# Retention's output product: the third and fourth column pairs each in two banks of the other PSUM pool, all four pairs in the wide form

## The chip, the cores and the metric

The kernel runs on one core of one Trainium2 chip. The metric is device time in microseconds (us) of one execution, the median over several runs. A profile is one execution taken by the hardware profiler: it gives every instruction with its engine, its line of the kernel, its tiles, its start and its duration.

## The reference

The reference is a trunk of four layers over 256 tokens of width 1024, batch 1. Each layer adds a token mixer and then a squared-ReLU MLP to the residual stream:

```python
for i in range(DEPTH):            # DEPTH = 4
    kind = i % N_MIXERS           # 0 retention, 1 convolution, 2 stick-breaking attention
    h = rms_norm(x, norm_mix[i])
    m = mixer[kind](h)
    x = x + m
    x = x + squared_relu_mlp(rms_norm(x, norm_ffn[i]), ffn_w1[i], ffn_w2[i])
return rms_norm(x, final_norm)
```

Retention is the mixer of layers 0 and 3. It ends with `return (jax.nn.silu(g) * y) @ w_out`, a product of a 256 x 2048 activation with a 2048 x 1024 weight. That product is the place of the change. It is followed in both layers by the MLP, whose first product is `h = relu(xn @ w1)` with a 1024 x 4096 weight.

## The kernel before, in words

Everything is float32. A float32 factor is split into a high part and a low part, and a product of two factors is taken as three partial products: high weight with high activation, high weight with low activation, low weight with high activation. Activations lie transposed: a tile of 128 partitions holds 128 features, its columns 0 to 255 are the high part of the 256 tokens, its columns 256 to 511 the low part.

**Weights** come in units of 512 KB (128 partitions x 1024). `unit` (L325) brings two units with one DMA on the SP queue into a `raw` tile, ScalarE casts the high part `wh` (L350, 128x1024), VectorE subtracts and leaves the low part `wl` (L357, 128x1024). `wh` and `wl` come from a pool of five buffers each (`wp`), taken in turn: the cast of a unit waits until TensorE has read the unit five places earlier for the last time. A unit of kind "b" holds four blocks of 128 rows by 256 columns, that is, one column pair (two output tiles of 128 features).

**Two forms** of a product on such a unit. The narrow form, `mm_b` (L490), makes three matmuls of 256 columns for each block of rows and each output tile (L504, L505, L506) and puts both output tiles of the pair into one PSUM bank. The wide form, `mm_w` (L509), makes two: the low weight with the 256 high columns (L520) and the high weight with all 512 columns at once (L524). It needs a bank for each output tile, since high and low part of the activation land in different halves; `sum_w` (L562) adds the halves afterwards: for each of the two banks a copy on ScalarE (L567) and an addition on VectorE (L568).

**PSUM** has eight banks here in two pools of four, `acc` and `mis`, each taken in turn. `acc` serves the large products; `mis` serves transposes, the attention products, column sums and broadcasts. A new tile waits until its bank has been read by all who read it before.

**The output product of retention** (L873 to L882): four column pairs, p = 0 to 3, each over 16 blocks of rows, which are four units (kb = 0 to 3). `OUT_ORDER` takes pairs 0 and 1 alternately through kb 0 to 3, and then pairs 2 and 3 the same way. Pairs 0, 1 and 2 are in the wide form with two `acc` banks each, pair 3 in the narrow form with one `acc` bank. When a pair is done, `evac` (L889) adds it to the residual x (L892), and `norm_pair` makes the two split activation tiles z of the next product (L439 on ScalarE, L440 on VectorE) and squares x (L450); GpSimd adds the squares up (L455).

**The MLP's first product** (`ffn`, L602) reads all eight z tiles; the last two, from pair 3, are here called z6 and z7. It has 16 pairs over two units each. In layer 0 all pairs are wide. In layer 3 the first two are narrow with one bank each and are evacuated only when the norm's factor is known; column sums (L400) give the mean square, VectorE finds its inverse root in eight small instructions (L469 and L384 to L395), and TensorE broadcasts it (L407). In layer 0 a sum over partitions (L480) takes that place.

**Order.** Most of the program's order is set by the compiler's scheduler, which simulates the engines and takes what it holds to be ready first; on each engine the instructions then run in that order. Only some matmuls are kept in program order by hand. A change in one place can therefore move instructions around it.

Of the kernel before, what the change touches and what calls it, by code (L numbers as in the profile page):

```python
# [242 lines left out]
class Trunk:  # L243
# [474 lines left out]
    def retention(self, j, nxt):  # L718
# [4 lines left out]
        q, k = [], []  # L723
        cosb, sinb = self.b2(self.c("cos", S)), self.b2(self.c("sin", S))
        for h in range(RH):
            for isk in range(2):
                if j == h == 0:
                    if not isk:
                        first = self.pairs_qk("ret_w_in", j, 0)
                    ps = first[isk]  # L730
                else:
                    ps = (self.pair_w if j else self.pair_b)("ret_w_in", j, isk * D + h * DK, self.zs)
# [55 lines left out]
        for h in range(RH):  # L788
            pv = [self.acc(), self.acc()]
            for kb in range(4):  # L790
                w = self.unit(("ret_w_in", j, "a", kb, 2 * D + h * DV))
# [14 lines left out]
            ps = self.mis()  # L806
# [18 lines left out]
        y = []  # L825
        for h in range(RH):
# [29 lines left out]
            for kb in range(4):  # L856
                w = self.unit(("ret_w_in", j, "a", kb, 4 * D + h * DV))
# [15 lines left out]
        evac = self.out_begin(nxt)  # L873
        ps = {}
        for kb, p in OUT_ORDER:
            w = self.unit(("ret_w_out", j, "b", kb, p * 256))
            two = p < 3
            if kb == 0:
                ps[p] = (self.acc(), self.acc()) if two else self.acc()
            (self.mm_w if two else self.mm_b)(ps[p], w, lambda k: y[k], kb * 4, kb == 0, kb == 3)  # L880
            if kb == 3:
                evac(p, self.sum_w(ps[p]) if two else ps[p])  # L882


    def out_begin(self, nxt, bias=None):
# [674 lines left out]
```

## Time and profile before

| what | value |
|---|---|
| runs of the kernel before | 1341.48, 1343.08, 1344.0 us (median 1343.08) |
| the profiled execution, first to last instruction (span) | 1340.3 us |
| median of the runs minus that span | 2.8 us |
| granted TensorE clock, mean | 0.999 |
| TensorE (PE) busy | 1330.8 us, 99% |
| VectorE (DVE) busy | 984.0 us, 73% |
| ScalarE (ACT) busy | 781.3 us, 58% |
| GpSimd (POOL) busy | 134.0 us, 10% |

The time of the profiled execution is known as its span only; the runs are 1.2 to 3.7 us longer than it.

A row of the timeline reads: start in us from the span's start, duration in us from the first to the last of the merged instructions, engine, line, operation, output tile <- input tiles, shape, how many instructions (x4), and in brackets the idle time before it and who ended that. Matmuls are pipelined: their durations overlap, and what one costs TensorE is the distance from its start to the next one's start. PEld rows are the weight loads of the matmuls.

### The profile page before, as it was taken

What the parts mean: (1) busy time and instruction counts of PE and PEld (TensorE: products, weight loads), DVE (VectorE), ACT (ScalarE), POOL (GpSimd) and SP (SyncE); (2) the same over time, 40 slices, a digit from 0 to 9 for tenths busy, and PEclk for the clock granted to TensorE, in tenths of its full rate; (3) what the DMA queues carried; (4) which work ended last, traced back from release to release, by engine and by line L of the source; (5) the groups of instructions that cost most, each with busy time, mean ns of one, the idle gap of its engine ahead of it and who ended that gap; (6) DMA issues with size and microseconds to landing.
All of it is one profiled execution on the core that took longest, in us unless ns stands there. A gap on an engine that the chain in (4) does not pass through costs nothing.

```text
span 1340.3 us, 20902 instructions
## 1 busy us (share of the span) xinstructions
PE 1330.8 (99%) x8285; PEld 1170.4 (87%) x8285; DVE 984.0 (73%) x1642; ACT 781.3 (58%) x1205; POOL 134.0 (10%) x123
## 2 busy tenths in 40 slices
PE   9999999999999999999999999999999999999998
PEld 7988888888999998888878898888888888988886
DVE  6977769775688698765687587755697777788643
ACT  7555546664457477744578577744565555555442
POOL 3200002000169210000100010000120000100000
PEclk9999999999999999999999999999999999999999
DMA  7555555555545645555453345555555454555551
GB/s 283 210 184 190 187 181 197 189 188 189 188 159 145 219 170 203 190 192 192 172 183 126 126 166 190 192 190 194 177 181 187 174 188 173 189 189 189 204 188 63
DMA packets 41586, 244.56 MB, mean 182 GB/s; under 512 B 4624, under 2 KB 9104, under 8 KB 14096
## 3 DMA queue, kind: packets, MB, share of 16 engines
q1 hardware_dynamic: 40768, 240.86, 50.7%
q10 hardware_dynamic: 720, 2.36, 0.5%
q8 instruction: 65, 1.06, 0.3%
q14 instruction: 33, 0.27, 0.1%
HBM read 241.27 MB, written 1.93 MB: 181 GB/s over the span
## 4 chain that ended last, share of the span: by engine, by line
PE 99%; DMA 0%; ACT 0%; DVE 0%; issue 0%; SPq 0%
PE acc L524 34%; PE acc L520 18%; PE acc L683 6%; PE acc L918 6%; PE acc L920 6%; PE acc L919 6%; PE acc L504 4%; PE acc L505 4%; PE acc L506 4%; PE acc L1087 1%; PE acc L1220 1%; PE mis L809 1%; PE mis L870 1%; PE mis L400 0%; PE mis L1458 0%; PE acc L585 0%
## 5 line engine op out<-in xcount | busy, mean ns | idle before, releaser
L357 DVE TENSOR_TENSOR wl<-raw,wh 128x1024 fp32r<-128x1024 f32 (+1 forms) x440 | 546.5, 1247 | 242.8 <-ACT wh L350 236.4
L350 ACT CAST wh<-raw 128x1024 fp32r<-128x1024 f32 (+1 forms) x440 | 456.5, 1042 | 353.1 <-PE acc L524 164.8
L524 PE MATMUL acc<-z,wh 128*128 128x512 f32 x1120 | 387.4, 392 | 0.0
L520 PE MATMUL acc<-z,wl 128*128 128x256 f32 x1120 | 310.2, 281 | 0.0
L524 PE MATMUL acc<-big,wh 128*128 128x512 f32 x864 | 298.8, 392 | 0.0
L524 PEld LDWEIGHTS acc<-z,wh 128*128 128x128 f32 x1120 | 208.3, 187 | 44.7
L520 PE MATMUL acc<-big,wl 128*128 128x256 f32 x864 | 238.5, 280 | 0.5 <-DVE t L568 0.5
L520 PEld LDWEIGHTS acc<-z,wl 128*128 128x128 f32 x1120 | 211.1, 189 | 1.7
L524 PEld LDWEIGHTS acc<-big,wh 128*128 128x128 f32 x864 | 161.0, 187 | 34.8
L520 PEld LDWEIGHTS acc<-big,wl 128*128 128x128 f32 x864 | 162.4, 189 | 2.3 <-DVE t L568 1.3
L918 PE MATMUL acc<-wh,z 128*128 128x512 f32 x352 | 138.0, 392 | 0.0
L920 PE MATMUL acc<-wh,z 128*128 128x512 f32 x352 | 137.3, 390 | 0.0
L919 PE MATMUL acc<-wl,z 128*128 128x512 f32 x352 | 137.2, 390 | 0.0
L455 POOL TENSOR_TENSOR t<-t,t 128x512 f32<-128x512 f32 x23 | 36.2, 1573 | 893.7 <-ACT t L450 850.6
L567 ACT COPY t<-acc 128x256 f32<-128x256 f32 x176 | 61.8, 373 | 100.6 <-PE acc L524 99.3
L568 DVE TENSOR_TENSOR t<-acc,t 128x256 f32<-128x256 f32 x176 | 69.1, 421 | 34.9 <-ACT t L567 34.8
L683 PE MATMUL acc<-wh,big 128*128 128x512 f32 x256 | 79.3, 390 | 0.0
L920 PEld LDWEIGHTS acc<-wh,z 128*128 128x128 f32 x352 | 66.1, 188 | 14.7 <-issue 0.8
L918 PEld LDWEIGHTS acc<-wh,z 128*128 128x128 f32 x352 | 66.1, 188 | 14.1 <-issue 0.8
L919 PEld LDWEIGHTS acc<-wl,z 128*128 128x128 f32 x352 | 66.1, 188 | 13.1
L504 PE MATMUL acc<-z,wh 128*128 128x256 f32 x256 | 72.5, 284 | 0.0
L505 PE MATMUL acc<-z,wh 128*128 128x256 f32 x256 | 72.4, 283 | 0.0
(259 smaller groups left out, 1813.0 us busy)
## 6 DMA issues: line engine op xcount, KB each, us to landing
raw<-in_w SPq DMA_DIRECT2D x214, 1024.0 KB, 4.8
raw<-in_w SPq DMA_DIRECT2D x8, 512.0 KB, 8.9
big<-in_gn SPq DMA_DIRECT2D x16, 256.0 KB, 5.2
raw<-hd SPq DMA_DIRECT2D x8, 263.0 KB, 4.8
raw<-hd SPq DMA_DIRECT2D x8, 131.5 KB, 3.6
x<-in_x SPq DMA_DIRECT2D x4, 256.0 KB, 6.3
wh<-in_w ACTq DMA_DIRECT2D x2, 512.0 KB, 6.4
wl<-in_w ACTq DMA_DIRECT2D x2, 512.0 KB, 8.5
```

The lines of the kernel that those rows point to most:

```text
L350: nc.scalar.copy(hi[:, s], src[:, s])
L357: self.nc.vector.tensor_sub(lo[:, s], src[:, s], hi[:, s])
L504: nc.tensor.matmul(o, wh[:, kk, cs], ah, start=st, stop=False, **kw)
L505: nc.tensor.matmul(o, wh[:, kk, cs], al, start=False, stop=False, **kw)
L520: mm = nc.tensor.matmul(ps[m][:, :S], wl[:, kk, cs], a[:, :S], start=first and kk == 0, stop=False, **kw)
L524: nc.tensor.matmul(ps[m], wh[:, kk, cs], a, start=False, stop=last and kk == 3, **kw)
L567: nc.scalar.copy(o[:, s], ps[m][:, S:])
L568: nc.vector.tensor_add(o[:, s], ps[m][:, :S], o[:, s])
L683: self.tc.keep_in_program_order(nc.tensor.matmul(ps[t], l, r[:, kk], start=False, stop=kb * 2 + kk == 31 and n == 2, **kw))
L918: nc.tensor.matmul(ps[t], zh[:, s], wh[:, kk], start=k == 0, stop=False, skip_group_check=True)
L919: nc.tensor.matmul(ps[t], zh[:, s], wl[:, kk], start=False, stop=False, skip_group_check=True)
L920: nc.tensor.matmul(ps[t], zl[:, s], wh[:, kk], start=False, stop=k == 7, skip_group_check=True)
```

## The change

Pair 3 is computed in the wide form as the others are. Pairs 0 and 1 keep two `acc` banks each; pairs 2 and 3 take two `mis` banks each. Nothing else in the source differs.

```diff
         for kb, p in OUT_ORDER:
             w = self.unit(("ret_w_out", j, "b", kb, p * 256))
-            two = p < 3
             if kb == 0:
-                ps[p] = (self.acc(), self.acc()) if two else self.acc()
-            (self.mm_w if two else self.mm_b)(ps[p], w, lambda k: y[k], kb * 4, kb == 0, kb == 3)
+                bank = self.acc if p < 2 else self.mis
+                ps[p] = bank(), bank()
+            self.mm_w(ps[p], w, lambda k: y[k], kb * 4, kb == 0, kb == 3)
             if kb == 3:
-                evac(p, self.sum_w(ps[p]) if two else ps[p])
+                evac(p, self.sum_w(ps[p]))
```

The scheduler's order differs around this place in layers 0 and 3 on TensorE, VectorE and ScalarE, up to the fourth pair of the MLP's first product; the rows of GpSimd and of the SP queue stand as before. Names with numbers are tiles: `acc_` and `mis_` are PSUM banks, `wh_` and `wl_` a unit's high and low part, `big_` the split activations of the output product, `z_` those of the MLP.

First place, TensorE in layer 0, the end of pairs 0 and 1 (`acc_1766`, `acc_1767`, `acc_1788`, `acc_1789`) and the start of pair 2 (1968 and 1969). Before:

```order
L524 MATMUL acc_1766<-big_1757,wh_1892 128x512
L524 MATMUL acc_1767<-big_1757,wh_1892 128x512
L524 MATMUL acc_1788<-big_1757,wh_1926 128x512
L524 MATMUL acc_1789<-big_1757,wh_1926 128x512
L520 MATMUL acc_1968<-big_1331,wl_1965 128x256
L524 MATMUL acc_1968<-big_1331,wh_1964 128x512
```

Of the change:

```order
L520 MATMUL mis_1968<-big_1331,wl_1965 128x256
L524 MATMUL mis_1968<-big_1331,wh_1964 128x512
L520 MATMUL mis_1969<-big_1331,wl_1965 128x256
L524 MATMUL mis_1969<-big_1331,wh_1964 128x512
L520 MATMUL mis_1968<-big_1334,wl_1965 128x256
L524 MATMUL mis_1968<-big_1334,wh_1964 128x512
L520 MATMUL mis_1969<-big_1334,wl_1965 128x256
L520 MATMUL acc_1766<-big_1748,wl_1893 128x256
```

Before, pair 2 began behind the last matmul of pairs 0 and 1, in the bank of pair 0. Now it begins ahead of the last quarter of pairs 0 and 1, in banks of the other pool.

Second place, VectorE in layer 0, at the first pair of the MLP's first product, whose banks are `acc_2192` and `acc_2193` before and `acc_2166` and `acc_2167` in the change. Before (`wl_2341` is the second unit of the MLP's third pair, and its five-places-earlier unit is `wl_2197`, the first of the first pair):

```order
L440 SCALAR_TENSOR_TENSOR z_2182<-x_119,prm_90,z_2182 128x256
L440 SCALAR_TENSOR_TENSOR z_2185<-x_119,prm_90,z_2185 128x256
L357 TENSOR_TENSOR wl_2341<-raw_2312,wh_2340 128x1024
L568 TENSOR_TENSOR t_438_2236<-acc_2192,t_438_2236 128x256
L568 TENSOR_TENSOR t_438_2236<-acc_2193,t_438_2236 128x256
```

Of the change (`wl_2354` is the first unit of the fourth pair, and its five-places-earlier unit is `wl_2191`, the second of the first pair):

```order
L568 TENSOR_TENSOR t_428_2150<-mis_1990,t_428_2150 128x256
L568 TENSOR_TENSOR t_428_2150<-mis_1991,t_428_2150 128x256
L892 TENSOR_TENSOR x_119<-t_428_2150,x_119 128x512
L357 TENSOR_TENSOR wl_2315<-raw_2286,wh_2314 128x1024
L440 SCALAR_TENSOR_TENSOR z_2156<-x_119,prm_90,z_2156 128x256
L440 SCALAR_TENSOR_TENSOR z_2159<-x_119,prm_90,z_2159 128x256
L357 TENSOR_TENSOR wl_2354<-raw_2351,wh_2353 128x1024
L568 TENSOR_TENSOR t_440_2210<-acc_2166,t_440_2210 128x256
L568 TENSOR_TENSOR t_440_2210<-acc_2167,t_440_2210 128x256
```

The preparation of weights now stands one unit further ahead where the first pair's evacuation comes. On TensorE at the same place, before, the last matmuls of the first pair (2192, 2193) were followed by nine matmul pairs of the second pair and L480, and then by the third pair in new banks; of the change:

```order
L524 MATMUL acc_2166<-z_2159,wh_2190 128x512
L524 MATMUL acc_2167<-z_2159,wh_2190 128x512
L520 MATMUL acc_2225<-z_2159,wl_2250 128x256
L524 MATMUL acc_2225<-z_2159,wh_2249 128x512
L520 MATMUL acc_2226<-z_2159,wl_2250 128x256
L524 MATMUL acc_2226<-z_2159,wh_2249 128x512
L480 MATMUL mis_2293<-t_432_2164,cst 128x256
L520 MATMUL acc_2284<-z_1918,wl_2289 128x256
```

Two matmul pairs and L480 now stand between the first pair's end and the third pair, whose bank `acc_2284` is that of `acc_2166`.

Third place, VectorE in layer 3, the inverse root of the norm's factor (its input is L400's sum, its result `ry` is L407's input). Before:

```order
L357 TENSOR_TENSOR wl_12259<-raw_12211,wh_12258 128x1024
L469 TENSOR_SCALAR rm_12136<-mis_12131 128x2
L384 TENSOR_SCALAR ry_12138<-rm_12136 128x2
L388 TENSOR_TENSOR rt_12139<-ry_12138 128x2
L389 SCALAR_TENSOR_TENSOR rt_12139<-rt_12139,rm_12136 128x2
L390 SCALAR_TENSOR_TENSOR rt_12139<-rt_12139 128x2
L391 SCALAR_TENSOR_TENSOR ry_12138<-rt_12139,ry_12138 128x2
L357 TENSOR_TENSOR wl_12298<-raw_12295,wh_12297 128x1024
L393 TENSOR_TENSOR rt_12139<-ry_12138 128x2
L357 TENSOR_TENSOR wl_12318<-raw_12295,wh_12317 128x1024
L394 SCALAR_TENSOR_TENSOR rt_12139<-rt_12139,rm_12136 128x2
L395 SCALAR_TENSOR_TENSOR ry_12138<-rt_12139,ry_12138 128x2
```

Of the change:

```order
L357 TENSOR_TENSOR wl_12246<-raw_12243,wh_12245 128x1024
L469 TENSOR_SCALAR rm_12084<-mis_12079 128x2
L357 TENSOR_TENSOR wl_12266<-raw_12243,wh_12265 128x1024
L384 TENSOR_SCALAR ry_12086<-rm_12084 128x2
L388 TENSOR_TENSOR rt_12087<-ry_12086 128x2
L389 SCALAR_TENSOR_TENSOR rt_12087<-rt_12087,rm_12084 128x2
L390 SCALAR_TENSOR_TENSOR rt_12087<-rt_12087 128x2
L391 SCALAR_TENSOR_TENSOR ry_12086<-rt_12087,ry_12086 128x2
L357 TENSOR_TENSOR wl_12305<-raw_12302,wh_12304 128x1024
L393 TENSOR_TENSOR rt_12087<-ry_12086 128x2
L394 SCALAR_TENSOR_TENSOR rt_12087<-rt_12087,rm_12084 128x2
L395 SCALAR_TENSOR_TENSOR ry_12086<-rt_12087,ry_12086 128x2
```

Two weight subtractions stand between L469 and L395 in both. What moved is which units they are: the subtraction ahead of L469 is now of `wl_12246`, and its five-places-earlier unit (`wh_12051`, `wl_12052`) is read by TensorE up to the second row before L400. On TensorE, 38 narrow matmuls and four wide matmul pairs stood between L400 and L407 before; 11 narrow matmuls and four wide pairs stand there in the change.

## The prediction

> **What bounds the kernel now.** I read the page first, then the waits of TensorE, then the timeline around the two retention layers.
>
> ```profile
> span 1340.3 us, 20902 instructions
> PE 1330.8 (99%) x8285; PEld 1170.4 (87%) x8285; DVE 984.0 (73%) x1642; ACT 781.3 (58%) x1205; POOL 134.0 (10%) x123
> PE 99%; DMA 0%; ACT 0%; DVE 0%; issue 0%; SPq 0%
> PE mis L292 <- POOL t L270: 1.3, 1, 1.3
> PE mis L1394 <- ACT big L1464: 1.0, 1, 1.0
> PE acc L585 <- ACT wh L350: 0.6, 1, 0.6
> PE acc L520 <- DVE t L568: 0.5, 2, 0.2
> ```
>
> TensorE is busy 99% of the span and is 99% of the chain that ended last. The last four rows are all that it waits for: 3.4 us in the whole program. So there is little waiting to win, any matmul time saved counts in full, and any wait that TensorE does not have today is paid in full. The last of these rows is the only wait inside the change. It comes twice, once in each retention layer:
>
> ```profile
> 182.86 1.09 PE L524 MATMUL acc<-big,wh 128*128 128x512 f32 x4
> 184.18 0.38 PE L520 MATMUL acc<-big,wl 128*128 128x256 f32 x1 [0.23 <-DVE t L568]
> 192.26 0.28 PE L504 MATMUL acc<-big,wh 128*128 128x256 f32 x1
> 197.89 0.28 PE L506 MATMUL acc<-big,wl 128*128 128x256 f32 x1
> 198.01 0.28 PE L520 MATMUL acc<-big,wl 128*128 128x256 f32 x1
> 201.25 0.28 PE L520 MATMUL acc<-big,wl 128*128 128x256 f32 x1
> 203.83 0.40 PE L524 MATMUL acc<-big,wh 128*128 128x512 f32 x1
> 204.06 0.28 PE L504 MATMUL acc<-big,wh 128*128 128x256 f32 x1
> 206.94 0.28 PE L520 MATMUL acc<-z,wl 128*128 128x256 f32 x1
> 209.77 0.52 PE L520 MATMUL acc<-z,wl 128*128 128x256 f32 x3
> ```
>
> **What the change removes.** *The wait for pair 0's bank.* The four L524 from 182.86 take TensorE 4 x 0.23 us (0.23 is 203.83 to 204.06), so pair 2 could start at 183.79; it starts at 184.18. In the change pair 2 has banks of its own pool, last read by the attention products long before: 0.39 us gone, 0.78 in two layers.
>
> *The narrow form.* From 192.26 to 198.01 run 48 narrow matmuls: 0.120 us each, 0.359 for the three of one block and output tile. From 201.25 to 204.06 run eight wide pairs: 0.351 each. Pair 3 has 16 blocks and two tiles, 32 such groups a layer, 64 in all: 64 x 0.008 = 0.5 us. The durations of the rows (0.28 three times against 0.28 and 0.40) would promise far more, but they overlap; starts count. Bounds: eight wide pairs from 206.94 to 209.77 take 0.354 each (0.3 us in all); the nine from 215.06 to 218.18, below, 0.347 (0.8 us).
>
> The Trainium skill, "TensorE: Matmul & The Clock Gate", section "Back-to-back issue gap", gives N/2.4 + 2.5 ns between starts at full clock: an estimate from it is 327 ns for three narrow and 325 for a wide pair, so 0.15 us instead of 0.5. The rows show 359 and 351, and they decide.
>
> **What it adds.** Four ScalarE copies and four VectorE additions in all, 0.37 and 0.42 us each by the page. They delay z6 and z7. In the change 24 wide pairs (8.4 us) stand between the MLP's start and the first read of z6 in layer 0, and 64 narrow matmuls (7.7 us) in layer 3. VectorE's path to z6 is set by the subtraction ahead of it, whose buffer is free after the MLP's first unit: 2.8 + 0.4 for that unit, 1.04 cast, 1.25 subtraction, 0.76 for z6 (mean of L440, 46.5 us over 64), 6.3 us. It fits, so I cost them at nothing; without the cover one copy and one addition a layer would show, 0.8 us each time.
>
> ```profile
> L357 DVE TENSOR_TENSOR wl<-raw,wh 128x1024 fp32r<-128x1024 f32 (+1 forms) x440 | 546.5, 1247 | 242.8 <-ACT wh L350 236.4
> L350 ACT CAST wh<-raw 128x1024 fp32r<-128x1024 f32 (+1 forms) x440 | 456.5, 1042 | 353.1 <-PE acc L524 164.8
> L567 ACT COPY t<-acc 128x256 f32<-128x256 f32 x176 | 61.8, 373 | 100.6 <-PE acc L524 99.3
> L568 DVE TENSOR_TENSOR t<-acc,t 128x256 f32<-128x256 f32 x176 | 69.1, 421 | 34.9 <-ACT t L567 34.8
> L440 DVE SCALAR_TENSOR_TENSOR z<-x,prm,z 128x256 fp32r<-128x256 f32 x64 | 46.5, 763 | 5.7 <-ACT z L439 5.7
> ```
>
> **What it moves, layer 0.** These rows are the end of the MLP's first pair before:
>
> ```profile
> 214.48 0.39 PE L524 MATMUL acc<-z,wh 128*128 128x512 f32 x1
> 214.91 0.72 ACT L567 COPY t<-acc 128x256 f32<-128x256 f32 x2 [3.84 <-PE acc L524]
> 215.31 0.77 DVE L568 TENSOR_TENSOR t<-acc,t 128x256 f32<-128x256 f32 x2 [0.86 <-ACT t L567]
> 215.06 0.28 PE L520 MATMUL acc<-z,wl 128*128 128x256 f32 x1
> 218.18 0.59 PE L480 MATMUL mis<-t,cst 128*128 128x256 f32 x2
> 218.42 0.47 PE L520 MATMUL acc<-z,wl 128*128 128x256 f32 x1
> 212.14 5.25 POOL L939 TENSOR_TENSOR big<-cst,prm 128x512 f32<-128x512 f32 x4
> 212.39 2.07 DVE L357 TENSOR_TENSOR wl<-raw,wh 128x1024 fp32r<-128x1024 f32 x1
> L939 POOL TENSOR_TENSOR big<-cst,prm 128x512 f32<-128x512 f32 x18 | 28.1, 1590 | 16.3 <-PE acc L506 16.3
> ```
>
> The first pair's last matmul of bank one starts at 214.48, the copies follow at 214.91, the additions at 215.31, and TensorE reaches the third pair only at 218.42: the evacuation has some 2.7 us to spare. In the change the third pair takes the first pair's own bank and only two wide pairs and L480 lie between. Count from R, the start of the first pair's last matmul. TensorE is due at 0.23 + 2 x 0.35 + 0.24 (218.18 to 218.42) = 1.17 us. But on VectorE the subtraction of `wl_2354` stands ahead of the evacuation, and its cast needs the buffer of `wh_2190`, which that very last matmul reads: 0.40 for the matmul, 1.04 cast, 1.25 subtraction, 0.42 addition = 3.11. TensorE, in order, waits 1.9 us at `acc_2284`. Everything behind it waits too, since nothing on TensorE is ready out of turn.
>
> The subtraction may cost more: GpSimd's four L939 come right after its norm sums, and the subtraction at 212.39 that ran among them took 2.07. The sums now end later, since x of pair 3 is squared some 2 to 3 us later, and the four L939 then cover the subtraction of `wl_2354`. With 2.07 the wait is 2.8. I take 2.5, nearer to the row that ran among L939.
>
> The Trainium skill, "SBUF — State Buffer", section "Who interferes with whom", says that a VectorE instruction with two SBUF inputs and a GpSimd instruction that reads SBUF block each other for the whole instruction. The 2.07 against the mean 1.25 agrees; by the rule the subtraction could wait a full L939, 1.59 by its row, the stall would be 3.5 and the time 1.0 us above my sum.
>
> **What it moves, layer 3.**
>
> ```profile
> 1161.68 0.95 PE L400 MATMUL mis<-cst,t 128*128 128x1 f32 x8
> 1162.49 0.36 PE L505 MATMUL acc<-z,wh 128*128 128x256 f32 x1
> 1168.55 0.61 PE L407 MATMUL mis<-cst,ry 128*128 128x128 f32 x4
> 1162.67 0.16 DVE L469 TENSOR_SCALAR rm<-mis 128x2 f32<-128x2 f32 x1 [1.76 <-PE mis L400]
> 1163.65 0.16 DVE L391 SCALAR_TENSOR_TENSOR ry<-rt,ry 128x2 f32<-128x2 f32 x1
> 1164.02 1.23 DVE L357 TENSOR_TENSOR wl<-raw,wh 128x1024 fp32r<-128x1024 f32 x1 [0.20 <-ACT wh L350]
> 1165.16 0.15 DVE L393 TENSOR_TENSOR rt<-ry 128x2 f32<-128x2 f32 x1
> 1166.80 0.16 DVE L395 SCALAR_TENSOR_TENSOR ry<-rt,ry 128x2 f32<-128x2 f32 x1
> ```
>
> Before, VectorE was idle when L400's sum came (1162.67), had the root at 1166.96, 5.3 us after L400's start, and TensorE reached L407 6.9 us after it: 1.6 to spare. In the change TensorE is due at L407 after 0.81 (L400) + 0.20 + 10 x 0.12 + 4 x 0.35 = 3.6 us, since only 11 narrow matmuls and four pairs stand between. VectorE is later, not earlier: ahead of L469 stands the subtraction of `wl_12246`, whose cast needs a buffer that TensorE reads until just before L400. From L400's start: cast 1.04, subtraction 1.25, L469 0.2, subtraction 1.14 (1164.02 to 1165.16), five small ones 1.0 (0.20 each, 1162.67 to 1163.65), subtraction 1.14, three small ones 0.6 = 6.4. TensorE waits 2.75 us at L407. Queued behind it is all of the MLP's third pair. The bounds, with the steps as tight as the nearest rows allow or each 0.1 longer, are 2.4 and 3.0; GpSimd has nothing to do there.
>
> **The sum.** Gains 0.78 + 0.5 = 1.3; new waits 2.5 + 2.75 = 5.25; net 3.95 us slower. Against the profiled execution: 1340.3 becomes 1344.2 as a span. The runs' median is 2.8 above the span, so 1347.0. Extremes: 4.3 - 1.6 = +2.7 and 5.8 - 1.1 = +4.7, that is 1345.8 to 1347.8, and with the runs' own scatter (1.6 down, 0.9 up) 1344.2 to 1348.7.
>
> **The rivals.** *Neither wait comes; not slower.* If both casts got their buffers earlier than the order of reads says, the evacuation and the root would be in time, and only the gains stay: 1341.8, no change that can be told. What decides is whether five buffers make the two casts wait: with 1.9 us more lead in layer 0 and 2.8 in layer 3 the waits are gone. For it speaks that the trace of before has no such wait; against it, that ScalarE's casts wait for TensorE through the whole trace (164.8 us in L350's row). 8%.
>
> *Only one of the two*, as when other casts in layer 3 lie earlier than I read: 1344.3 to 1344.5, within the resolution. 13%.
>
> *The wide form is worth its instruction count.* If the durations counted, 64 groups would save 64 x (0.85 - 0.68) = 11 us and the time were about 1336 with the waits. The starts from 192.26 on speak against it. 3%.
>
> *A third wait.* In layer 0 the fourth pair's bank is freed on VectorE after the reciprocal and two more subtractions, all pushed back with the first wait; I find under 0.3 us to spare. If these also fall under GpSimd's work, another 1 to 2 us: 1348.5. 8%.
>
> **How the numbers follow.** My forecast has 68%. A measurement of this kernel tells some 0.2% from no change, 2.7 us. The forecast's lower edge touches that, so slower gets 0.70, same 0.26 (the first two rivals and that edge), faster 0.04. The range reaches down to the single wait, with scatter, and up to the third wait: 1343.7 to 1349.0.
>
> **What would show it.** In the changed profile: the two 0.2 us waits for L568 at pair 2 gone; pairs 2 and 3 at 0.35 us a wide pair; a wait of about 2.5 us of TensorE for L568 about 11 us into layer 0's MLP, with L357 and L350 just ahead of it; one of about 2.75 us for L395 at L407 in layer 3. If TensorE waits at neither, the prediction is wrong in its main step; if z6 is waited for, I priced the additions wrong.

## The result, and the profile after

The changed kernel takes 1344.78 us, the median of 21 runs (1341.84 to 1347.29), the kernel before 1342.23 us, the median of 21 runs beside them (1341.30 to 1344.14). The ratio is 1.0014, with a 95% interval of 1.0009 to 1.0020. So the change makes the kernel slower, by some 1.9 us by the ratio and 2.55 us by the medians, which is below the 0.2%, 2.7 us, that the prediction took as what a measurement tells: by that measure the outcome is the "same" to which it gave 0.26, and slower only by the 21 runs' interval. The times of the changed kernel also spread more, over 5.4 us where the kernel before has 2.8, and this turned out to be the key to them.

The head of the page of the changed kernel, with its busy times and the chain that ended last:

```profile
span 1341.9 us, 20781 instructions
PE 1330.1 (99%) x8221; PEld 1166.8 (87%) x8221; DVE 981.9 (73%) x1646; ACT 782.1 (58%) x1209; POOL 134.1 (10%) x123
PE 95%; DMA 1%; POOL 1%; ACT 1%; issue 1%; DVE 1%; SPq 0%; POOLq 0%; ACTq 0%; DVEq 0%
```

TensorE is still the bound. The waits that the view lists (us in total, times, longest):

```profile
PE acc L585 <- ACT wh L350: 1.5, 1, 1.5
PE mis L407 <- DVE ry L395: 1.5, 1, 1.5
PE mis L292 <- POOL t L270: 1.3, 1, 1.3
PE mis L1394 <- ACT big L1464: 1.0, 1, 1.0
PE mis L407 <- DVE lns L1149: 0.3, 1, 0.3
PE acc L1220 <- DMA wl<-in_w: 0.2, 1, 0.2
```

The two waits for L568 at pair 2 are gone. The wait at L407 for L395, in layer 3, is there, with 1.5 us instead of 2.75. A wait for L568 in layer 0, forecast at 2.5 us, is not in this list. The first row is at the program's start, where it came out anywhere from 0.3 to 1.6 us in the profiles of this study; the stretches compared below begin behind it.

**Layer 0.** The timeline of the changed kernel about 10 us into the MLP (start, us, engine, line, operation, count, and in brackets the idle time before with its releaser):

```profile
213.20 0.40 PE L524 MATMUL acc<-z,wh 128*128 128x512 f32 x1
213.68 1.05 ACT L350 CAST wh<-raw 128x1024 fp32r<-128x1024 f32 x1 [1.17 <-issue]
214.76 1.25 DVE L357 TENSOR_TENSOR wl<-raw,wh 128x1024 fp32r<-128x1024 f32 x1 [1.79 <-ACT wh L350]
214.89 4.05 POOL L939 TENSOR_TENSOR big<-cst,prm 128x512 f32<-128x512 f32 x3
216.89 0.65 ACT L567 COPY t<-acc 128x256 f32<-128x256 f32 x2 [2.17 <-PE acc L524]
217.30 0.76 DVE L568 TENSOR_TENSOR t<-acc,t 128x256 f32<-128x256 f32 x2 [1.28 <-ACT t L567]
217.61 0.59 PE L480 MATMUL mis<-t,cst 128*128 128x256 f32 x2
217.86 0.47 PE L520 MATMUL acc<-z,wl 128*128 128x256 f32 x1
```

The prediction had the cast wait for the first pair's last matmul. It ran at 213.68, 3 us ahead of that matmul and 0.08 us after the matmul at 213.20 had ended, which is the last to read another unit. VectorE then stood idle for 1.28 us ahead of the additions, and the third pair followed L480 without a gap.

One pair later something small stands that the list of waits does not show:

```profile
222.69 0.48 DVE L375 CAST big<-t 128x256 fp32r<-128x256 f32 x2
223.09 0.74 DVE L568 TENSOR_TENSOR t<-acc,t 128x256 f32<-128x256 f32 x2
223.37 0.39 PE L524 MATMUL acc<-z,wh 128*128 128x512 f32 x1
223.62 0.19 PEld L520 LDWEIGHTS acc<-z,wl 128*128 128x128 f32 x1 [0.17 <-issue]
223.65 0.35 PE L520 MATMUL acc<-z,wl 128*128 128x256 f32 x1
223.84 0.40 PE L524 MATMUL acc<-z,wh 128*128 128x512 f32 x1
```

From 223.37 to 223.84 a pair's two starts take 0.47 us, where 0.35 is usual: 0.12 us lost at the first matmul of the MLP's fourth pair. The first of the two additions at 223.09 ends at 223.50, just ahead of the late weight load at 223.62. It reads the second pair's first bank. The same row of the kernel before:

```profile
220.27 0.74 DVE L568 TENSOR_TENSOR t<-acc,t 128x256 f32<-128x256 f32 x2
```

There the third pair began at 218.42, so the fourth at about 218.42 + 16 x 0.347 = 223.97, and the first addition, done at 220.68, had 3.3 us to spare. Now the reciprocal and a subtraction stand ahead of the additions on VectorE.

**Layer 3.** The same view around the root chain:

```profile
1161.87 1.05 ACT L350 CAST wh<-raw 128x1024 fp32r<-128x1024 f32 x1 [1.30 <-issue]
1162.95 1.23 DVE L357 TENSOR_TENSOR wl<-raw,wh 128x1024 fp32r<-128x1024 f32 x1 [1.91 <-ACT wh L350]
1164.50 0.28 PE L506 MATMUL acc<-z,wl 128*128 128x256 f32 x1
1164.74 0.95 PE L400 MATMUL mis<-cst,t 128*128 128x1 f32 x8
1165.73 0.16 DVE L469 TENSOR_SCALAR rm<-mis 128x2 f32<-128x2 f32 x1 [1.56 <-PE mis L400]
1165.81 1.21 DVE L357 TENSOR_TENSOR wl<-raw,wh 128x1024 fp32r<-128x1024 f32 x1
1168.13 0.40 PE L524 MATMUL acc<-z,wh 128*128 128x512 f32 x1
1168.16 1.22 DVE L357 TENSOR_TENSOR wl<-raw,wh 128x1024 fp32r<-128x1024 f32 x1 [0.27 <-ACT wh L350]
1169.68 0.16 DVE L395 SCALAR_TENSOR_TENSOR ry<-rt,ry 128x2 f32<-128x2 f32 x1
1169.99 0.68 PE L407 MATMUL mis<-cst,ry 128*128 128x128 f32 x4 [1.46 <-DVE ry L395]
```

VectorE was idle for 1.56 us ahead of L469, so no late subtraction held the chain up at its head: the one ahead of L469 ran at 1162.95, from a cast at 1161.87, although TensorE read the unit five places earlier until the matmul at 1164.50. But two subtractions stand in its middle (1165.81 and 1168.16), the root is there 5.1 us after L400's start, and TensorE was due 3.6 us after it.

**The program in five stretches.** The starts of five matmul groups on TensorE cut the program into stretches. Of the kernel before (218.18, L480, stands in the prediction) and of the changed one (its L480 is at 217.61, above):

```profile
124.08 1.03 PE L870 MATMUL mis<-cst,t 128*128 128x128 f32 x8
436.26 0.61 PE L400 MATMUL mis<-cst,big 128*128 128x1 f32 x4
684.05 1.03 PE L1394 MATMUL mis<-cst,t 128*128 128x128 f32 x8
1122.39 1.03 PE L870 MATMUL mis<-cst,t 128*128 128x128 f32 x8
1245.27 1.03 PE L669 MATMUL acc<-cst,x 128*128 128x128 f32 x8
```

```profile
124.54 1.03 PE L870 MATMUL mis<-cst,t 128*128 128x128 f32 x8
435.81 0.61 PE L400 MATMUL mis<-cst,big 128*128 128x1 f32 x4
684.95 1.03 PE L1394 MATMUL mis<-cst,t 128*128 128x128 f32 x8
1123.20 1.03 PE L870 MATMUL mis<-cst,t 128*128 128x128 f32 x8
1246.79 1.04 PE L669 MATMUL acc<-cst,x 128*128 128x128 f32 x8
```

Differences of these starts, and the same for the kernels of the experiments below, one profiled execution each (us). L870 comes in four groups a layer: the first stretch begins at the first of layer 0's, the last stretch at the last of layer 3's, so the first has a part of the attention in it.

| kernel | layer 0, output product to L480 | rest of layer 0's MLP | convolution | layer 2 and layer 3's attention | layer 3, output product and MLP |
|---|---|---|---|---|---|
| before | 94.10 | 218.08 | 247.79 | 438.34 | 122.88 |
| before, second profile | 94.09 | 218.09 | 248.61 | 438.28 | 122.88 |
| changed | 93.07 | 218.20 | 249.14 | 438.25 | 123.59 |
| changed, second profile | 93.07 | 218.22 | 248.75 | 438.25 | 123.59 |
| layer 0 alone | 93.07 | 220.85 | 248.54 | 438.24 | 122.82 |
| layer 3 alone | 94.09 | 218.09 | 248.71 | 438.28 | 124.01 |
| banks alone | 93.75 | 218.09 | 248.55 | 438.34 | 122.52 |
| changed, later broadcast | 93.08 | 220.87 | 249.29 | 438.23 | 122.33 |
| layer 0 alone, longer wait | 93.07 | 221.21 | 249.05 | 438.77 | 122.79 |
| layer 0 alone, bank for the fourth pair | 93.07 | 218.10 | 248.89 | 438.54 | 122.86 |
| changed, bank for the fourth pair | 93.07 | 218.09 | 248.46 | 438.54 | 123.63 |
| changed, both | 93.07 | 218.04 | 248.90 | 438.55 | 122.38 |
| mixed (layer 0 changed, bank for its fourth pair; layer 3 banks alone) | 93.07 | 218.09 | 249.17 | 438.54 | 122.51 |
| before, one matmul more | 94.09 | 218.31 | 248.64 | 438.30 | 122.82 |

The first two stretches repeat to 0.02 us (once 0.05) wherever their part of the program is the same. The last two repeat to 0.1 us, or differ by a quarter of a us and more for a reason found below; the convolution scatters. That makes them a finer measure than the times. Three things stand out. Layer 0's output product gains 1.0 us wherever layer 0 has the whole change. The convolution costs more in every profile than in the first one of the kernel before. And the rest of layer 0's MLP has two values, 218.1 and 220.9 (221.2 where a wait was made longer).

### The profile page after: what moved, and what is told of

Read it like the earlier page. It is cut to its first block, busy times and chain, and to the rows that moved or that the text cites. A ratio compares the mean times of both kernels' runs of the same rounds, so it can differ in the third digit from the quotient of the medians.

```text
span 1341.9 us, 20781 instructions
## 1 busy us (share of the span) xinstructions
PE 1330.1 (99%) x8221; PEld 1166.8 (87%) x8221; DVE 981.9 (73%) x1646; ACT 782.1 (58%) x1209; POOL 134.1 (10%) x123
## 3 DMA queue, kind: packets, MB, share of 16 engines
q8 instruction: 64, 1.05, 0.3%
## 4 chain that ended last, share of the span: by engine, by line
PE 95%; DMA 1%; POOL 1%; ACT 1%; issue 1%; DVE 1%; SPq 0%; POOLq 0%; ACTq 0%; DVEq 0%
PE acc L524 33%; PE acc L520 17%; PE acc L683 6%; PE acc L918 6%; PE acc L920 6%; PE acc L919 6%; PE acc L504 3%; PE acc L505 3%; PE acc L506 3%; PE mis L524 2%; PE mis L520 1%; POOL big L1016 1%; DMA wl<-in_w 1%; PE acc L1087 1%; PE acc L1220 1%
## 5 line engine op out<-in xcount | busy, mean ns | idle before, releaser
L524 PE MATMUL acc<-z,wh 128*128 128x512 f32 x1120 | 387.4, 392 | 0.0
L524 PE MATMUL acc<-big,wh 128*128 128x512 f32 x800 | 277.2, 392 | 0.0
L524 PEld LDWEIGHTS acc<-z,wh 128*128 128x128 f32 x1120 | 208.3, 187 | 44.7
L520 PE MATMUL acc<-big,wl 128*128 128x256 f32 x800 | 222.0, 280 | 0.0
L524 PEld LDWEIGHTS acc<-big,wh 128*128 128x128 f32 x800 | 149.3, 187 | 32.7
L520 PEld LDWEIGHTS acc<-big,wl 128*128 128x128 f32 x800 | 150.6, 189 | 0.7
L568 DVE TENSOR_TENSOR t<-acc,t 128x256 f32<-128x256 f32 x172 | 67.3, 421 | 36.9 <-ACT t L567 36.8
```

The source lines that it names most:

```text
L520: mm = nc.tensor.matmul(ps[m][:, :S], wl[:, kk, cs], a[:, :S], start=first and kk == 0, stop=False, **kw)
L524: nc.tensor.matmul(ps[m], wh[:, kk, cs], a, start=False, stop=last and kk == 3, **kw)
L568: nc.vector.tensor_add(o[:, s], ps[m][:, :S], o[:, s])
```

## The experiments

Two theories came out of the two traces. **Theory A**: the parts add up (layer 0 gives 1.0 us, layer 3's wait costs 1.5), and the 1.35 us that the convolution lost is scatter of that layer, which sends data out and back by DMA. **Theory B**: the convolution's loss is a consequence of the change. A theory C in the texts below puts the whole loss, 1.0014, on one layer. The one that held was formed after the first four runs.

### The change by layer, and by part

One layer at a time (shown for layer 0; for layer 3 the condition is `j == 1`):

```diff
+            new = j == 0
+            two = new or p < 3
             if kb == 0:
-                bank = self.acc if p < 2 else self.mis
-                ps[p] = bank(), bank()
+                bank = self.mis if new and p > 1 else self.acc
+                ps[p] = (bank(), bank()) if two else bank()
```

> The change in layer 0 alone; layer 3 as before. Both theories: the two waits for L568 at layer 0's pair 2 gone, no wait at the MLP's third pair, TensorE at layer 0's norm 0.6 us earlier by the span's clock (1.0 us against the start-up). Theory A (the 1.5 us that the convolution layer lost in the changed profile is scatter of that layer's transfers and of GpSimd): the time falls by 1.0 us, ratio 0.999 to 0.9995, and the convolution of this profile loses nothing or something else than 1.5 us. Theory B (the loss follows from layer 0 ending earlier): the convolution loses 1.5 us again, ratio 1.000 to 1.0005. Theory C (layer 0 carries the whole loss): ratio 1.0014.

> The change in layer 3 alone; everything up to layer 3 is the kernel before. Both theories: TensorE waits about 1.5 us for L395 at L407 in layer 3, the wait for L568 at that layer's pair 2 is gone, and layer 3 as a whole costs 0.5 to 0.7 us. Theory A and B: ratio 1.0004 to 1.0006, and the convolution as in the profile of before up to its scatter; if it moves here by 1 us or more although nothing ahead of it is changed, that is scatter (A). Theory C': layer 3 carries the whole loss, ratio 1.0014.

Layer 0 alone: 1343.82 us, ratio 1.0003 (0.9994 to 1.0012), above the 0.999 to 0.9995 that theory A expected. Its 11 times lie in two groups with nothing between: five from 1341.15 to 1341.93, six from 1343.82 to 1345.20. The profiled execution, 1343.82, is of the upper group, and its rest of the MLP takes 220.85 us instead of 218.09. Layer 3 alone: 1344.06 us, ratio 1.0011 (1.0002 to 1.0020), where 1.0004 to 1.0006 was expected; all 11 times lie within 1.4 us. The wait at L407 is there with 1.5 us, and its last stretch takes 124.01 us, 1.13 more than before and 0.42 more than in the changed kernel. Its convolution took 248.71 us although nothing ahead of it was changed, 0.92 more than in the first profile. So the convolution speaks for A, and C is out for layer 0; layer 3's interval has 1.0014 in it, but its stretches have only the 1.13 us. No theory had foreseen the two groups.

The banks without the wide form, in both layers:

```diff
             two = p < 3
             if kb == 0:
-                ps[p] = (self.acc(), self.acc()) if two else self.acc()
+                bank = self.acc if p < 2 else self.mis
+                ps[p] = (bank(), bank()) if two else bank()
```

> Pairs 2 and 3 in banks of the other pool in both layers, pair 3 narrow as before (one bank, no copy, no addition). Theory A and B: the two waits of 0.39 us are gone and nothing else is moved, since L400 keeps 38 narrow matmuls and four pairs behind it: no wait at L407, 0.8 us faster, ratio 0.9994. Rival: the move to the other pool delays that pool's other users (transposes, norm sums) and gives the gain back: ratio 1.0000 or more with a new wait for a bank of the other pool.

Measured: 1341.40 us (1340.43 to 1342.54), ratio 0.9991 (0.9982 to 1.0000). The stretches give 0.34 in layer 0 and 0.36 in layer 3. No wait at L407. The bank's part of the prediction was right. The rest of layer 0's gain, 93.75 to 93.07, is the wide form, with what it does to the pace of the other wide pairs.

### The later broadcast

```diff
-            if k == (2 if last else 0):
+            if k == (4 if last else 0):
```

> The change as it is, with layer 3's broadcast L407 four wide pairs (1.4 us) further back in the MLP's third pair; the same matmuls. Theory A and B (the wait at L407 is paid in full, and is only the root's chain against TensorE's arrival): the wait falls from 1.5 to 0.1 us or less, and the time by 1.4 us against the changed kernel, ratio 1.0004 to the kernel before. Rival: the two held pairs' activations start later, the banks for the MLP's fourth pair come free later, and a wait of 1 us or more appears at its first matmul: ratio stays 1.0014.

Measured: 1344.63 us (1341.45 to 1346.82), ratio 1.0013 (1.0004 to 1.0022), no better than the changed kernel. By the times, the rival. By the trace, not: the wait at L407 is gone, no other took its place, and layer 3's stretch is 122.33 us, 1.26 less than in the changed kernel and 0.55 less than before. What hides this gain is the rest of layer 0's MLP again, 220.87 us.

### What the upper group is

Matmuls L524 on TensorE from 230 to 350 us, inside layer 0's MLP (window, length, busy time and count of matmuls and of weight loads, granted clock, DMA share, GB/s), of the kernel before, of layer 0 alone, and of layer 0 alone with the bank of the next experiment:

```profile
230.00:350.00 120.00, 120.00 (x347) 64.70 (x346) 1.00 0.54 193
```

```profile
230.00:350.00 120.00, 120.00 (x341) 63.98 (x340) 1.00 0.54 190
```

```profile
230.00:350.00 120.00, 120.00 (x348) 64.76 (x347) 1.00 0.54 192
```

The clock is 1.00 in all three, nothing waits, and yet one of them does six or seven wide pairs fewer in 120 us. From the starts, a pair takes 346.7 ns in the first and third, with a steady 116 or 117 and 230 between its starts. In the second it takes 353.3 ns, and the steps vary (113 to 121 for the narrow matmul). Some 400 pairs follow from the fourth pair to the MLP's end, and 400 x 6.6 ns = 2.64 us: the distance of the two groups, and, with the 0.12 us of the short wait, that of 220.85 from 218.09. In the kernel of layer 0 alone the pairs run at 346.7 ns up to the short wait ahead of the fourth pair, between 222.31 and 222.78 us, and at the slow rate from 223.0 us on. That gave **theory D**: VectorE's additions of the second pair come too late by 0.1 us, and after this wait TensorE runs the wide pairs at 353 ns in a part of the executions. Its rival, **E**, put the groups down to the convolution's transfers.

The fourth MLP pair of layer 0 gets two banks of the other pool, so that it does not depend on those additions:

```diff
-    def pair_w(self, name, l, c0, acts, nkb=2, **keep):
+    def pair_w(self, name, l, c0, acts, nkb=2, bank=None, **keep):
         nc = self.nc
-        ps = [self.acc(), self.acc()]
+        bank = bank or self.acc
+        ps = [bank(), bank()]
...
+                bank = self.mis if i == 0 and p == 3 else self.acc
-                act(self.pair_w(*pw, keep=p >= (2 if last else 4), before=factor if at else None))
+                act(self.pair_w(*pw, bank=bank, keep=p >= (2 if last else 4), before=factor if at else None))
```

This was put on layer 0 alone, on the changed kernel with the later broadcast, and on a mixed kernel (layer 0 as changed; in layer 3 the banks alone). It also moves work: half of the fourth pair now runs ahead of the third.

> The change in layer 0 alone, and that layer's fourth MLP pair in two banks of the other pool, so that it does not wait for VectorE's additions of the second pair. Theory D (the additions of the second pair end 0.1 us too late, and after this wait TensorE's wide pairs run at 353 instead of 347 ns in a part of the executions, to the end of layer 0's MLP, 2.7 us): no idle time ahead of the fourth pair, 347 ns from 220 to 360 us, one group of times instead of two, at 1341.2 to 1342, ratio 0.999 to 0.9995. Rival E (the two groups come from the convolution layer's transfers): the groups stay, 1341.5 and 1344.4, ratio 1.0003.

> The whole change, with layer 3's broadcast four wide pairs later and layer 0's fourth MLP pair in banks of the other pool. Theory D: neither wait, 347 ns in layer 0's MLP, one group of times; layer 0 gives 1.0 us and layer 3 some 0.5 us: 1340.8, ratio 0.9990. Rival E: no better than the same kernel without the other bank, 1344.6, ratio 1.0013 and spread over 5 us.

> Layer 0 as changed with its fourth MLP pair in banks of the other pool; in layer 3 the banks of the other pool, but the fourth column pair narrow as before, so that L400 keeps its 38 narrow matmuls behind it. Theory D: layer 0 gives 1.0 us, layer 3 its 0.4 us for the bank, no wait at L407: 1340.8, ratio 0.9990, one group of times. Rival E: two groups, 1341 and 1344, ratio 1.0000.

Layer 0 alone with it: 1342.39 us, ratio 1.0000 (0.9991 to 1.0009). The two groups are gone: the times run from 1341.84 to 1344.21, as those of the kernel before beside them do (1341.45 to 1343.99). The gap ahead of the fourth pair is gone, the rate is 346.7 ns. The ratio expected, 0.9990 to 0.9995, was missed: of the gain of 1.0 us the profile gives back 0.28 us in the convolution and 0.26 in the stretch behind it (against the second profile of the kernel before), and the rest is within the interval. The 0.26 is no scatter: it stands in all four kernels with this bank, and the last section shows where. The changed kernel with both: 1341.33 us (1340.93 to 1342.26), ratio 0.9990 (0.9981 to 0.9999), 3.3 us below the same kernel without the bank, **faster than the changed kernel**, and faster than the kernel before by an interval that only just leaves out 1. The mixed one: 1341.95 us (ten times of 1341.46 to 1342.23 and one of 1344.50), ratio 0.9996 (0.9987 to 1.0004), where 0.9990 was expected. E is out: the convolution was left as it was and the groups went. D is not the only reading left, since the bank also changes the order of the third and fourth pair; no run takes the wait away and keeps the order.

> The changed kernel once more. Theory D: two groups of times, 1341.8 to 1343.7 and 1344.3 to 1347.3; where the profiled execution shows layer 0's MLP at 353 ns a wide pair from the fourth pair on it belongs to the upper group, where it shows 347 to the lower; the short idle time ahead of the fourth pair in both. Rival E: the rate in layer 0's MLP and the group do not go together.

Measured: 1345.00 us, ratio 1.0014 (1.0006 to 1.0023); four times of 1342.42 to 1343.71, seven of 1344.96 to 1346.74. The profiled execution is one of the lower four, 1342.50, and runs at 346.7 ns, behind the same short wait. So the wait does not force the slow rate; behind it either rate can follow.

### A longer wait, and a break without a wait

On layer 0 alone, VectorE reads the second pair's first bank once more (`extra` is set for layer 0's second pair only; the lines that pass it on are left out):

```diff
-    def sum_w(self, ps):
+    def sum_w(self, ps, extra=False):
...
             nc.vector.tensor_add(o[:, s], ps[m][:, :S], o[:, s])
+            if extra and m == 0:
+                nc.vector.tensor_copy(self.tmp()[:, :S], ps[0][:, :S])
```

> The change in layer 0 alone, and VectorE reads the second MLP pair's first bank once more (one copy of 128x256, 0.3 to 0.4 us) right behind its addition, so that the wait ahead of the fourth pair grows from 0.1 to 0.4 or 0.5 us; nothing else is moved. Theory D (after any such wait the wide pairs may run at 353 ns): two groups of times 2.7 us apart, 1341.8 and 1344.8, ratio 1.0005. Theory D' (only a wait so short that it ends within a pair does it; after a longer one the pairs run at 347): one group at 1341.8, ratio 0.9995. Rival (VectorE's lateness costs by itself, the rate has no part in it): one group some 0.4 us above the one of layer 0 alone.

Measured: 1343.54 us, ratio 1.0012 (1.0003 to 1.0020); six times of 1342.33 to 1343.54 and five of 1344.42 to 1345.76. The profiled execution, 1345.32, is of the upper group and runs at 353.3 ns. Its timeline:

```profile
222.04 0.41 DVE L568 TENSOR_TENSOR t<-acc,t 128x256 f32<-128x256 f32 x1
222.32 0.39 PE L524 MATMUL acc<-z,wh 128*128 128x512 f32 x1
222.37 0.41 DVE L570 COPY t<-acc 128x256 f32<-128x256 f32 x1
222.92 0.36 PE L520 MATMUL acc<-z,wl 128*128 128x256 f32 x1 [0.21 <-DVE t L570]
```

The added copy (L570) is all that the source adds, and TensorE now waits for it by name: 222.32 to 222.92 is 0.60 us where 0.23 is usual. That shows that the fourth pair's first matmul waits for VectorE's last read of the second pair's first bank. The two groups and the rate are as theory D has them; D', that a longer wait is followed by the fast rate alone, is out. The longer wait did not make the upper group larger (five of 11, after six of 11).

Then the kernel before, with one matmul of a single column (two instructions in the trace) between the third and the fourth pair, `tick` being set for layer 0's fourth pair only:

```diff
         ps = [self.acc(), self.acc()]
+        if tick:
+            self.colsum(ps[0][:, :1], self.id, self.sc(1024))
```

> The kernel before, with one matmul of one column, 0.1 to 0.2 us, put between layer 0's third and fourth MLP pair; it waits for nothing. Theory D1 (any break in the row of wide pairs lets the rate fall): a second group of times 2.7 us above, or all executions there, ratio up to 1.002, and 353 ns in layer 0's MLP of a profile of that group. Theory D2 (it takes a wait for another engine): one group, 0.1 to 0.2 us above the kernel before, ratio 1.0001, 347 ns.

Measured: 1343.18 us (1341.91 to 1343.93), ratio 1.0005 (0.9996 to 1.0014), one group; the profile has 346.7 ns and 0.22 us more in the MLP's stretch. So a break in the row of pairs without a wait brought no second group of times and no slow rate in the one profile, as D2 has it. The medians stand 0.9 us apart; the profile shows only the 0.22, and the interval covers both. A few executions at 353 ns would not stand out in these times, and this kernel is the one before, with its own order, so the test is a weak one.

### Scatter, and the price of layer 3's wait

> The kernel before once more, for a second profile. Theory A (the 0.8 to 1.4 us that the convolution layer costs more in every later profile than in the first one of the kernel before is scatter of that layer): from 430 to 500 us this profile is 0.8 to 1.4 us behind the first, though the program is the same, ratio 1.0000. Theory B (the loss comes with the changes): this profile is within 0.2 us of the first there.

Measured: 1342.23 us, ratio 0.9999 (0.9990 to 1.0008). Its convolution took 248.61 us, 0.82 more than in the first profile of the same program. So A holds: the first profile of the kernel before was a favourable one. All others lie between 248.46 and 249.29, and no loss in the convolution beyond its scatter is shown for the change.

Last, the changed kernel with only the bank for the fourth pair:

> The whole change with only layer 0's fourth MLP pair in banks of the other pool; layer 3's broadcast stays where the change has it. Theory D: the 1.5 us wait for L395 at L407 is there and is paid in full, layer 0's MLP runs at 347 ns: one group of times at 1342.4 to 1343, 1.1 to 1.7 us above the same kernel with the later broadcast, ratio to the kernel before 1.0001 to 1.0005. Rival (L407's wait is absorbed later): as with the later broadcast, 1341.3, ratio 0.9990.

Measured: 1342.58 us (1342.04 to 1343.58), ratio 1.0000 (0.9991 to 1.0009), one group. The wait is there:

```profile
PE mis L407 <- DVE ry L395: 1.5, 1, 1.5
```

Against the same kernel with the later broadcast, 1341.33 us, it costs 1.25 us by the medians (the kernel before had 1342.61 and 1342.52 beside the two), and by the stretches 123.63 - 122.38 = 1.25. The wait is paid in full but for 0.2.

## Why the prediction was right, and where it was not

The direction and the range held, in part by luck. Of the two waits of the sum one came, at half its size. What else made the kernel slower, the slow rate in layer 0's MLP, is no term of the sum; without it the changed kernel would stand at some 1342.0 (1342.23 less the 0.2 us worked out below), under the range and no slower than before. The changed kernel with the bank for the fourth pair, whose profile shows no slow rate there, measured 1342.58, the kernel before beside it 1342.61.

- **The bound.** Right: what TensorE gains or waits in a stretch, the times show (1.25 us at L407 in both).
- **Pair 0's bank, 0.39 us a layer.** Right: 0.34 and 0.36.
- **The wide form, 0.25 us a layer.** Mis-sized: 0.68 in layer 0 and 0.19 in layer 3 (122.52 to 122.33, where L407 takes 0.08 more). The prediction took one rate from eight pairs (0.351) and saw a second (0.354 and 0.347) only as an uncertainty of the reading. They are two rates that hold for long stretches, and the trace of before had more of them: from this row to 192.26, a row that the prediction shows, stand 22 wide pairs of pair 2 itself, 0.347 each.

```profile
184.64 0.28 PE L520 MATMUL acc<-big,wl 128*128 128x256 f32 x1
```

At 0.347 the 32 groups of pair 3 are worth 0.40 us. The other 0.28 of layer 0's 0.68 is the pace of the 128 wide pairs that both kernels have: they average 353 ns with the banks alone and 351 in the changed kernel.
- **The copies and additions are hidden.** Right: no wait for z6 or z7.
- **The wait of 2.5 us at the MLP's third pair in layer 0.** Wrong, by its step "its cast needs the buffer of `wh_2190`". The five weight buffers are not given out in strict turn, as the text ahead of the prediction says they are: the cast ran 0.08 us after another unit's last reader ended. That it took the buffer that came free first is read from these times and was not shown by itself; no kernel with a sixth buffer was run. GpSimd's part failed too. The subtraction at 214.76 ran beside L939 from 214.89 and took 1.25 us, the mean of its row, not 2.07. This time it was first, and L939 was the one held up, 2.04 us where the next took 1.05:

```profile
214.89 2.04 POOL L939 TENSOR_TENSOR big<-cst,prm 128x512 f32<-128x512 f32 x1
216.89 1.05 POOL L939 TENSOR_TENSOR big<-cst,prm 128x512 f32<-128x512 f32 x1
```

By the Trainium skill, "SBUF — State Buffer", section "Who interferes with whom", the one that issues first holds up the other; these rows agree.
- **The wait of 2.75 us at L407.** Right in place and releaser, too large: 1.46 us. TensorE's arrival was right (3.6 us after L400). VectorE's chain took 5.1 us instead of 6.4, because the same wrong step had put a late subtraction ahead of L469; its cast ran at 1161.87, 2.9 us before the last read of the unit five places earlier ended.
- **The rivals of no wait (8%) and of one wait (13%).** Both casts did get their buffers earlier than the order of reads says, which is the first rival's condition, but only one of the waits went: the root's chain is too long for TensorE's 3.6 us even without the late subtraction. By the trace it is the second rival that came, one of the two waits; its 1344.3 to 1344.5 is the nearest number to 1344.78. But its example was layer 3's wait going, and it was layer 0's; and it priced the remaining wait at 2.5 to 2.75 us, so its number too is met only because the slow rate came.
- **The rival of a third wait**, "in layer 0 the fourth pair's bank is freed on VectorE after the reciprocal and two more subtractions", with "under 0.3 us to spare" and 8%. This is the wait that came, though the prediction let it depend on the first one. Its direct size is 0.12 us, not 1 to 2. What follows it costs more: 2.65 us of slower matmuls in a part of the executions.
- **The base.** The three runs shown had a median of 1343.08, the 21 runs later 1342.23. So 0.85 us of the forecast of 1347.0 was the base.

The sum as the runs have it: layer 0's output product -1.03, the short wait +0.12, layer 3 +0.71 (-0.55 without L407's wait, +1.26 for it): -0.2 us in an execution at 346.7 ns, +2.45 in one at 353.3. Of the 32 times of the changed kernel, 20 lie at 1344.3 us or above. If these ran at 353.3 ns, the mean should be 0.2 x 12 less and 2.45 x 20 more, over 32: +1.5 us. The means of the 21 runs each differ by 1.9 (1344.44 and 1342.54). The last 0.4 is not accounted for; the convolution alone scatters by 0.8.

What stays open is what sets the rate, and why that of 353.3 ns follows the short wait in a part of the executions and did not follow the added matmul. The rate of layer 3's output product differs between kernels too (353.0 ns with layer 3 alone, 347.3 in the changed kernel, and with it 124.01 and 123.59 us for the stretch).

## What to carry to other kernels

Where one engine is busy 99% of the time, a step that is put on a second engine has to be followed past the first consumer: the additions were in time for the third pair and 0.1 us late for the fourth, and it was the fourth that decided. Where a kernel's times fall into two groups, profile it more than once and compare the starts of the same instructions stretch by stretch; stretches that repeat to 0.02 us show at once which one has two values, and a gain that an unrelated stretch hides. And don't derive a wait from a pool by counting buffers in turn; look in the trace for when the like request was served.

## What the runs showed of the hardware that was not expected

Rows of wide pairs (a 128x256 and a 128x512 matmul) run at one of two rates at the same granted clock of 1.00: 346.7 ns a pair with steady steps, or 353.3 ns with steps that vary. In layer 0's MLP a rate, once there, held for 140 us. There four kernels, one of them run twice, had the short wait ahead of the fourth pair (0.12 us, or some 0.5 with the added copy). Of the 65 executions of these five sets 41 lie in the upper group of their times, and the five profiles agree with the groups: three at 353.3 ns in the upper, two at 346.7 in the lower. (In three of the five sets the groups are 1.25 to 2 us apart, with the later broadcast by a single low time; in the 21 times of the changed kernel and with the longer wait, where the other scatter blurs them, they are cut at 1344.) The nine profiles of kernels without this wait show 346.7 there.

Elsewhere in the same traces a wait is neither needed nor enough. A row of 37 wide pairs in layer 0's attention and the same row in layer 3, of the kernel before (first pair, and the matmul behind the last):

```profile
161.42 0.28 PE L520 MATMUL acc<-big,wl 128*128 128x256 f32 x1
174.49 0.28 PE L520 MATMUL acc<-big,wl 128*128 128x256 f32 x1
1109.44 0.28 PE L520 MATMUL acc<-big,wl 128*128 128x256 f32 x1
1122.27 0.28 PE L520 MATMUL acc<-big,wl 128*128 128x256 f32 x1
```

The first takes 353.1 ns a pair, within 0.1 in all 14 profiles, and TensorE waits for nothing right ahead of it. The second takes 346.7 here and, within 0.1, in eight other profiles, and 353.1 in five: the four kernels with the bank for the fourth pair and the one with the longer wait. The granted clock is 1.00 in both rows. 37 x 6.4 ns = 0.24 us is nearly all of the 0.26 that the fourth stretch costs more with that bank. And behind the 0.23 us wait for L568 at pair 2, in both layers of the kernel before, the pairs ran at 346.7.
